# A gMLP and sliding-window decoder trunk: first loads and first products in another order, spatial gating and row sums moved

## The chip, the cores and the metric

The kernel runs on one core of a Trainium2 chip. Its engines, as the profile names them: PE (TensorE) multiplies matrices and adds into banks of PSUM, PEld is PE's load of the stationary operand, DVE (VectorE) works elementwise on two operands, ACT (ScalarE) computes functions and copies, POOL (GpSimd) does elementwise work and masks, SP (SyncE) issues most transfers between HBM and SBUF. ACT issues a few. Each engine runs its instructions strictly in the order in which they were put, and waits for the others by semaphores.

The metric is the device time of one execution in microseconds (us), smaller is better. The times of the kernel before are given as a median of three runs.

## The reference

One batch of 1024 tokens, width 1024, all in float32, passes through two layers. What matters of it:

```python
def gmlp_mixer(h, w_in, ln_g, ln_b, w_s, b_s, w_out):       # layer 1
    u, v, z = jnp.split(h @ w_in, 3, axis=-1)               # 1024 -> 3 x 2048
    u = gelu(u)
    v = layer_norm(gelu(v), ln_g, ln_b)
    v = v.reshape(bsz, 8, 128, 8, 256)                      # chunks, tokens, groups, channels
    w_causal = where(tril, w_s, 0)
    s = einsum('gts,bnsgc->bntgc', w_causal, v) + b_s       # a 128x128 matrix per group
    return (u * s * silu(z)) @ w_out

# layer 1: h = x + rms_norm(gmlp_mixer(rms_norm(x)))
# then k, v = rms_norm(h) @ w_k, rms_norm(h) @ w_v
# layer 2: windowed attention with sinks and ALiBi, a SiLU gate, w_out, rms_norm, residual
```

The change touches layer 1 alone: the product that gives v, and the part that gives u and z with the spatial product s.

## The kernel before

**Products.** Each float32 operand is split into a high part of type fp32r and the low rest, also fp32r (ACT makes the high part, DVE the low). A product is the sum of three matmuls, high by high, high by low, low by high: `mm3` (lines 226 to 229), 128 rows by 512 columns into one PSUM bank. On top of that the layer's products are cut in 2 x 2 blocks, and the four blocks are got by seven products of sums of blocks, numbered m = 1 to 7. `T[m]` is the token side's operand of product m, in a high and a low tile; the weights' side is split piece by piece as it arrives.

**Stage 1, `v_layer` (lines 343 to 573, some 0 to 155 us).** It takes 28 steps n of a product m and half u of the inner dimension, in the order m = 1, 2, 5, 6, 7, 4, 3. A step multiplies two slices k of 128 rows (kk = 0, 1) with four slices t of 128 tokens, each a call of `mm3`, so 24 matmuls. The sums of product 1 stand in four banks `vb`, those of product 2 in four banks `vc`. Two steps ahead `prep` loads and splits. The first steps are written out by hand (lines 460 to 487): the first weight piece `r0` (`raw_v`) is loaded in halves of 512 columns, the token slices `xa` 0 and 1 each on its own, then 2 and 3 together, then the second weight piece `r1_`. ACT (line 471) writes the high part of `T[1]`, POOL (line 472) that of the weights, DVE the two low parts (lines 473 and 475). Behind them come the splits of slices 2 and 3 (`split_scaled`, lines 108 to 110) and of `r1_` (`split`, lines 104 to 106), and then the next operands. Line 386 (`t_prep`, m = 5) scales `xa` in place on ACT and is held behind the split of `r1_`. The piece called `whi<-vraw` in the trace (line 105, step 4) follows on ACT, and on DVE its low part (line 106).

**Stage 2, `uz_layer` (lines 576 to 812, some 155 to 497 us).** u and z are computed for eight groups g of 256 channels, a "quad" q for u (zz = 0) and one for z (zz = 1), 16 quads. A quad is seven products into three banks, `ub` (products 1, 2 in `ua`, 6, 7, 4) and `uc` (5 and 3). Its weights (`raw_uz`, two transfers) are split in three lots, `whi_g`/`wlo_g`, and two named `uzhilo_g` (from sums `f`, which POOL makes at line 264 when they are loaded). A group's z quad also holds the spatial product: `spatial(g, i, j)` (lines 680 to 690) multiplies four slices of the normalised v, `vg`, with the masked matrix `wc`, plain float32, 128x128 (tile `sp`, four matmuls in the program, each two passes in the trace). DVE then applies gain and offset `t1` (line 687) and multiplies u by it (line 264, `uz_slots<-uz_slots,sp`). `group_consts(g)` (lines 660 to 673) loads the next group's `vg` on SP (1 MB) and computes the row sums of `wc` in a bank `rb`: DVE clears it (line 667), PE multiplies with ones (line 668), DVE makes two tiles `t` of offsets (line 672). `normalise` (line 678) then subtracts the mean from `vg` and scales, eight slices on DVE.

The banks for `sp`, `rb`, `uc` and `ua` are four, in turn. The tile `vg` exists once: its next load waits until the matmuls of `sp` have read it. At the end of a product, `scale` multiplies with the tokens' factor `bc` on DVE (line 264, `uz_slots<-uz_slots,bc`), SiLU or GELU follows on ACT (lines 694 and 778), and the result goes out in transfers `td`. Between the steps of stage 2 a generator `presum` (lines 814 to 846) prepares sums of the second layer's weights: two loads `presum_raw`, five POOL additions (line 832), ACT and DVE splits (lines 840, 841), and a store `od` of 640 KB.

**What sets the order.** The program is written as a sequence of calls; a scheduler that knows dependencies sorts the instructions of each engine by a priority that follows this sequence, and lets some go ahead. What is tied by `tc.keep_in_program_order` stays as written. So a call at another place in the code can move instructions of several engines.

## Time and profile before

| | |
|---|---|
| median of 3 runs | 1029.4 us (1029.36 to 1029.69) |
| the profiled execution: its own time | 1029.93 us |
| its span, first to last instruction | 1028.2 us |
| PE busy | 1019.6 us, 99% of the span |
| DVE busy | 767.7 us, 75% |
| ACT busy | 512.9 us, 50% |
| POOL busy | 255.3 us, 25% |
| mean granted TensorE clock | 0.998 |

Busy is the time in which an engine has an instruction in execution. A matmul's record of 0.39 us overlaps the next one's: in the steady run the starts of two matmuls of 128x512 lie 0.227 us apart (22 rows from 12.20 to 16.96 us, without a wait). In the rows of the timeline, the number in front is the start in us, the next the duration, `xN` the number of instructions put together in the row, and a bracket says how long the engine had stood idle before it and what ended that.

### The profile page before, as it was taken

How to read it: one execution, taken by the hardware profiler on the slowest of the kernel's cores; microseconds unless marked ns; L12 is line 12 of the kernel's file. 1: busy time of each engine (PE TensorE's matmuls, PEld its weight loads, DVE VectorE, ACT ScalarE, POOL GpSimd, SP SyncE). 2: the span in 40 equal slices, each digit the busy share in tenths (PEclk: the TensorE clock that was granted, in tenths of full speed). 3: DMA queues.
4: the chain of work that ended last, by engine and by line, in shares of the span. 5: the costliest groups of instructions: out<-in, count | busy, mean ns of one | idle time of the engine just before them, and what ended most of it. 6: DMA issues, size and time to landing. Idle time of an engine off the chain costs nothing.

```text
span 1028.2 us, 14492 instructions
## 1 busy us (share of the span) xinstructions
PE 1019.6 (99%) x5186; PEld 837.6 (81%) x5186; DVE 767.7 (75%) x1317; ACT 512.9 (50%) x1013; POOL 255.3 (25%) x251
## 2 busy tenths in 40 slices
PE   9999999999999999999999999999999999999997
PEld 7888888888888888888888888888997777777776
DVE  6997467888888888988787678555147557877986
ACT  6694443645445444455445455344126345544752
POOL 0010004374653746634200000000000112225421
PEclk9999999999999999999999999999999999999999
DMA  8788243545544455556998652997135444415564
GB/s 310 269 294 294 103 167 113 160 154 170 190 158 154 150 162 193 166 169 227 324 386 319 206 188 69 328 374 274 53 120 199 149 150 163 144 52 191 214 250 177
DMA packets 117416, 203.83 MB, mean 198 GB/s; under 512 B 7776, under 2 KB 59872, under 8 KB 117344
## 3 DMA queue, kind: packets, MB, share of 16 engines
q1 hardware_dynamic: 112512, 193.17, 54.6%
q10 hardware_dynamic: 4512, 8.68, 2.4%
q8 instruction: 41, 0.67, 0.3%
q0 software_dynamic: 320, 1.05, 0.3%
q14 instruction: 31, 0.25, 0.1%
HBM read 142.05 MB, written 60.82 MB: 197 GB/s over the span
## 4 chain that ended last, share of the span: by engine, by line
PE 97%; POOL 1%; DMA 1%; issue 0%; DVE 0%; ACT 0%; SPq 0%; DVEq 0%; POOLq 0%; ACTq 0%
PE qz L227 6%; PE qz L229 6%; PE qz L228 6%; PE ub L227 6%; PE ub L229 6%; PE ub L228 6%; PE oc L227 3%; PE oc L229 3%; PE oc L228 3%; PE uc L227 3%; PE ob L228 3%; PE ob L227 3%; PE uc L229 3%; PE uc L228 3%; PE ob L229 3%; PE sp L685 3%
## 5 line engine op out<-in xcount | busy, mean ns | idle before, releaser
L1208 ACT ACTIVATE pr<-pr,mx 128x129 f32<-128x129 f32 x128 | 50.2, 394 | 58.5 <-DVE mx L1202 58.3
L227 PE MATMUL qz<-n_hi,whi_w 128*128 128x512 f32 x192 | 77.1, 402 | 0.0
L229 PE MATMUL qz<-n_hi,wlo_w 128*128 128x512 f32 x192 | 74.9, 390 | 0.0
L228 PE MATMUL qz<-n_lo,whi_w 128*128 128x512 f32 x192 | 74.9, 390 | 0.0
L110 DVE SCALAR_TENSOR_TENSOR wlo_w<-raw_w,gn,whi_w 128x512 fp32r<-128x512 f32 x40 | 28.7, 748 | 51.0 <-ACT whi_w L109 43.8
L832 POOL TENSOR_TENSOR presum<-presum_raw 128x128 f32<-128x128 f32 x80 | 41.6, 553 | 92.4 <-DMA od<-presum 85.5
L109 ACT ACTIVATE whi_w<-raw_w,gn 128x512 fp32r<-128x512 f32 x40 | 27.1, 717 | 65.4 <-PE pv L229 30.4
L106 DVE TENSOR_TENSOR uzhilo_g<-f,uzhilo_g 128x1024 fp32r<-128x1024 f32 x31 | 45.7, 1473 | 12.7 <-ACT uzhilo_g L105 12.7
L841 DVE TENSOR_TENSOR presum<-presum 128x128 fp32r<-128x128 f32 x80 | 50.6, 674 | 2.7 <-ACT presum L840 2.7
L227 PE MATMUL ub<-T,whi_g 128*128 128x512 f32 x128 | 50.8, 397 | 0.0
L227 PE MATMUL ub<-T,uzhilo_g 128*128 128x512 f32 x128 | 50.5, 394 | 0.0
L1229 POOL TENSOR_SCALAR_AFFINE_SELECT pc<-pc 128x1024 f32<-128x1024 f32 x16 | 20.1, 1259 | 122.1 <-DVE wlo_w L110 109.2
L229 PE MATMUL ub<-T,wlo_g 128*128 128x512 f32 x128 | 50.0, 390 | 0.0
L264 POOL TENSOR_TENSOR f<-raw_uz 128x512 f32<-128x512 f32 x15 | 20.3, 1354 | 119.4 <-DMA raw_uz<-in_wuz_in_dram 104.2
L229 PE MATMUL ub<-T,uzhilo_g 128*128 128x512 f32 x128 | 49.9, 390 | 0.0
L228 PE MATMUL ub<-T,whi_g 128*128 128x512 f32 x128 | 49.8, 389 | 0.0
L228 PE MATMUL ub<-T,uzhilo_g 128*128 128x512 f32 x128 | 49.8, 389 | 0.0
L227 PE MATMUL uc<-T,uzhilo_g 128*128 128x512 f32 x124 | 48.8, 394 | 0.0
L228 PE MATMUL uc<-T,uzhilo_g 128*128 128x512 f32 x124 | 48.4, 390 | 0.0
L229 PE MATMUL uc<-T,uzhilo_g 128*128 128x512 f32 x124 | 48.3, 389 | 0.0
L105 ACT ACTIVATE whi_g<-raw_uz 128x1024 fp32r<-128x1024 f32 (+1 forms) x31 | 26.4, 852 | 41.7 <-PE ub L228 13.8
L105 ACT ACTIVATE uzhilo_g<-f 128x1024 fp32r<-128x1024 f32 x31 | 32.7, 1055 | 27.6 <-PE uc L229 21.7
(408 smaller groups left out, 3228.4 us busy)
## 6 DMA issues: line engine op xcount, KB each, us to landing
raw_uz<-in_wuz_in_dram SPq DMA_DIRECT2D x32, 512.0 KB, 3.6
orawP2a<-td SPq DMA_DIRECT2D x28, 512.0 KB, 4.3
td<-uz_slots SPq DMA_DIRECT2D x52, 256.0 KB, 2.2
od<-presum SPq DMA_DIRECT2D x16, 640.0 KB, 4.0
raw<-in_wv_in_dram SPq DMA_DIRECT2D x17, 512.0 KB, 5.0
vg<-vd SPq DMA_DIRECT2D x8, 1024.0 KB, 5.6
orawP2b<-in_wo_a_dram SPq DMA_DIRECT2D x16, 512.0 KB, 7.5
raw_w<-in_wqz_dram SPq DMA_DIRECT2D x16, 512.0 KB, 5.8
```

The source lines that it names most:

```text
L105: nc.scalar.activation(hi, src, AF.Copy)
L106: nc.vector.tensor_tensor(lo, src, hi.bitcast(F32), ALU.subtract)
L109: nc.scalar.activation(hi, src, AF.Copy, scale=g)
L110: nc.vector.scalar_tensor_tensor(lo, src, g, hi.bitcast(F32), ALU.mult, ALU.subtract)
L227: nc.tensor.matmul(out, lhsT=a_hi, rhs=b_hi, start=start, stop=False, skip_group_check=True)
L228: nc.tensor.matmul(out, lhsT=a_hi, rhs=b_lo, start=False, stop=False, skip_group_check=True)
L229: nc.tensor.matmul(out, lhsT=a_lo, rhs=b_hi, start=False, stop=stop, skip_group_check=True)
L264: (eng or nc.vector).tensor_tensor(out, a, b, op)
L685: nc.tensor.matmul(psv[:, n], lhsT=d["vg"][:, 4 * j + n, i * P:(i + 1) * P], rhs=d["wc"], start=n == 0, stop=n == 3, skip_group_check=True)
L832: tc.keep_in_program_order(nc.gpsimd.tensor_tensor(o, a, b, op))
L841: tc.keep_in_program_order(nc.vector.tensor_tensor(t[:, k], lo[k], hi.bitcast(F32), ALU.subtract))
L1208: nc.scalar.activation(pr[:, i], pr[:, i], AF.Exp, bias=mx[:, i:i + 1], scale=-1.0, accum_out=dn[:, i:i + 1])
```

## The change

Four edits, all in layer 1.

1. The head of stage 1 loads in the order weight half 0, slice 0, weight half 1, slice 1, then `r1_` half 0, slice 2, `r1_` half 1, slice 3: eight transfers of 256 KB, where there were four of 256 KB and two of 512 KB in another order. The high part of `T[1]` for slices 0 and 1 is written by ACT in halves of 256 columns. The splits of `r1_` and of slices 2 and 3 alternate.
2. In steps n = 0 and 1 the matmuls of one slice k run part by part: first high by high for all four t, then the second part for all four, then the third. From n = 2 on the order is that of before (the sort by t gives it).
3. The four spatial products of a group stand together, behind product 6 of the z quad. Before, two stood there and two behind product 5.
4. `group_consts` only loads `vg`. The row sums, a new function `row_sums`, are taken right behind the four spatial products for the next group (and once at the start for group 0).

```diff
--- before.py
+++ after.py
@@ -462,25 +462,27 @@
         load(r0[:, 0:512], wv_in[0, 0][:, 0:512])
         xload(xa[:, 0], 0, 0, 0, 1)
         nc.scalar.activation(small[:, 4:5], ones[:, 0:1], AF.Gelu_apprx_tanh)
+        load(r0[:, 512:1024], wv_in[0, 0][:, 512:1024])
         xload(xa[:, 0], 0, 0, 1, 1)
-        load(r0[:, 512:1024], wv_in[0, 0][:, 512:1024])
-        xload(xa[:, 0], 0, 0, 2, 2)
+        r1_ = raws.take("v1")
+        for k in range(2):
+            load(r1_[:, k * 512:(k + 1) * 512], wv_in[0, 1][:, k * 512:(k + 1) * 512])
+            xload(xa[:, 0], 0, 0, 2 + k, 1)
         p0 = pieces.take("v0")
         for k in range(2):
             cs = slice(k * 512, k * 512 + 512)
-            nc.scalar.activation(T[1][0][:, k], xa[:, 0, k], AF.Copy, scale=g(0, k))
+            for ts_ in (slice(0, 256), slice(256, 512)):
+                nc.scalar.activation(T[1][0][:, k, ts_], xa[:, 0, k, ts_], AF.Copy, scale=g(0, k))
             nc.gpsimd.tensor_copy(p0[0][:, cs], r0[:, cs])
             nc.vector.scalar_tensor_tensor(T[1][1][:, k], xa[:, 0, k], g(0, k), T[1][0][:, k].bitcast(F32),
                                            ALU.mult, ALU.subtract)
             nc.vector.tensor_tensor(p0[1][:, cs], r0[:, cs], p0[0][:, cs].bitcast(F32), ALU.subtract)
         ready[0] = p0
-        r1_ = load(raws.take("v1"), wv_in[0, 1])
-        for k in range(2, 4):
-            split_scaled(T[1][0][:, k], T[1][1][:, k], xa[:, 0, k], g(0, k))
         ready[1] = pieces.take("v1")
         for k in range(2):
             cs = slice(k * 512, k * 512 + 512)
             split(ready[1][0][:, cs], ready[1][1][:, cs], r1_[:, cs])
+            split_scaled(T[1][0][:, 2 + k], T[1][1][:, 2 + k], xa[:, 0, 2 + k], g(0, 2 + k))
         first_split.append(list(nc.cur_bb.bb.instructions)[-2])
         xload(xb, 1, 0, 0, 2)
         prep(2)
@@ -503,10 +505,11 @@
             for kk in range(2):
                 k = 2 * u + kk
                 cs = slice(kk * 512, kk * 512 + 512)
-                for t in range(4):
-                    ts_ = slice(t * P, (t + 1) * P)
-                    mm3(ps[t], T[m][0][:, k, ts_], T[m][1][:, k, ts_], hi[:, cs], lo[:, cs],
-                        first and k == 0, k == HT - 1)
+                by_part = [(i, t) for i in range(3) for t in range(4)]
+                for i, t in by_part if n < 2 else sorted(by_part, key=lambda a: a[1]):
+                    a, b = (T[m][i // 2][:, k, t * P:(t + 1) * P], (hi, lo, hi)[i][:, cs])
+                    nc.tensor.matmul(ps[t], lhsT=a, rhs=b, start=first and k == 0 and i == 0,
+                                     stop=k == HT - 1 and i == 2, skip_group_check=True)
             if n >= 2 and (Q, m, u) != (0, 2, 1):
                 prep(n + 2)
             if n >= len(steps) - 3:
@@ -662,6 +665,9 @@
             d["vg"] = vg = big.tile([P, NB, 256], F32, tag="P1_2", name=f"vg{g}")
             src = vd[g // 2][:, :, g % 2 * 256:g % 2 * 256 + 256]
             nc.sync.dma_start(out=vg, in_=src.rearrange("n p c -> p n c"))
+
+        def row_sums(g):
+            d = grp[g]
             wc, bsb = d["wc"], d["bsb"]
             ps = bank("s", f"rb{g}")[:, 0:P]
             nc.vector.memset(ps, 0.0)
@@ -726,6 +732,7 @@
         four = big.tile([P, 4, TH], F32, tag="P1_3", name="uz_slots4")
         slots += [more[:, i] for i in range(6)] + [four[:, i] for i in range(4)]
         group_consts(0)
+        row_sums(0)
         fetch(1)
         prev = None
         for q in range(len(quads) + 1):
@@ -778,8 +785,11 @@
                     tc.keep_in_program_order(nc.scalar.activation(pc[at], pc[at], AF.Gelu_apprx_tanh))
             step(sums_b)
             if zz:
-                spatial(g, 0, 0)
-                spatial(g, 0, 1)
+                for i in range(2):
+                    for j in range(2):
+                        spatial(g, i, j)
+                if g + 1 < G:
+                    row_sums(g + 1)
                 if not last:
                     finish(g, 0, 0)
             else:
@@ -791,9 +801,6 @@
             step(sums_b)
             prep2(q + 1)
             fetch(q + 2)
-            if zz:
-                spatial(g, 1, 0)
-                spatial(g, 1, 1)
             product(q, 7, b, False)
             c[1, 1] = slot()
             copy(c[1, 1], b)
```

How this moves the rows of the engines, at three places. A number behind a tile's name (`sp_2970`) tells apart the tiles of one name, and differs between the two programs.

ACT at the head, `T_133` being the high part of `T[1]`, and `T_164` or `T_168` that of `T[2]`. First before, then the change:

```order
L471 ACTIVATE T_133<-xa,gn 128x512 x2
L109 ACTIVATE T_133<-xa,gn 128x512 x2
L105 ACTIVATE whi_v_157<-raw_v_151 128x512 x2
L386 ACTIVATE xa<-xa,gn 128x512
L109 ACTIVATE T_164<-xb,gn 128x512 x2
L386 ACTIVATE xa<-xa,gn 128x512
L105 ACTIVATE vhi_171<-raw_02_169 128x1024
L386 ACTIVATE xa<-xa,gn 128x512
```

```order
L475 ACTIVATE T_133<-xa,gn 128x256 x4
L105 ACTIVATE whi_v_157<-raw_v_140 128x512
L109 ACTIVATE T_133<-xa,gn 128x512
L105 ACTIVATE whi_v_157<-raw_v_140 128x512
L109 ACTIVATE T_133<-xa,gn 128x512
L386 ACTIVATE xa<-xa,gn 128x512 x2
L109 ACTIVATE T_168<-xb,gn 128x512 x2
L386 ACTIVATE xa<-xa,gn 128x512
L105 ACTIVATE vhi_175<-raw_02_173 128x1024
L386 ACTIVATE xa<-xa,gn 128x512
```

The scaling of line 386, which stood behind the split of `r1_`, still does, and `r1_` now comes between the last slices of `xa`; ACT has four smaller pieces for the first two slices, and the last piece of `T_133` is now behind the split of `r1_`. In the rows that follow, the fourth L386 stood behind the four copies `vslot`, and now stands ahead of them.

DVE in group 4 of stage 2, from the clearing of `rb` to the multiplication with `bc` (`vg_3051` and `vg_3062` are the v of group 5, which is loaded here; `sp_3019`, `sp_3026` and `sp_2981`, `sp_2988`, `sp_2995` are spatial products of group 4). Before, then the change:

```order
L667 MEMSET rb_3053 128x128
L106 TENSOR_TENSOR uzhilo_g_10_3010<-f_3006,uzhilo_g_10_3010 128x1024
L687 SCALAR_TENSOR_TENSOR sp_3019<-sp_3019,gn,t_41_2707 128x512
L687 SCALAR_TENSOR_TENSOR sp_3026<-sp_3026,gn,t_41_2707 128x512
L264 TENSOR_TENSOR uz_slots_1333<-uz_slots_1333,sp_3019 128x512
L264 TENSOR_TENSOR uz_slots<-uz_slots,sp_3026 128x512
L672 SCALAR_TENSOR_TENSOR t_50_3056<-rb_3053,gn,bsb_2824 128x128
L264 TENSOR_TENSOR uz_slots_1333<-uz_slots_1333,uc_2987 128x512
L672 SCALAR_TENSOR_TENSOR t_51_3058<-rb_3053,gn,bsb_2824 128x128
L264 TENSOR_TENSOR uz_slots_1333<-uz_slots_1333,bc 128x512
L678 TENSOR_SCALAR vg_3051<-vg_3051,mv,ve 128x256 x7
L264 TENSOR_TENSOR uz_slots_1333<-uz_slots_1333,uz_slots 128x512
```

```order
L673 MEMSET rb_3002 128x128
L264 TENSOR_TENSOR uz_slots<-uz_slots 128x512
L678 SCALAR_TENSOR_TENSOR t_50_3005<-rb_3002,gn,bsb_2828 128x128
L678 SCALAR_TENSOR_TENSOR t_51_3007<-rb_3002,gn,bsb_2828 128x128
L848 TENSOR_TENSOR presum<-presum 128x128 x3
L106 TENSOR_TENSOR uzhilo_g_10_3035<-f_3031,uzhilo_g_10_3035 128x1024
L684 TENSOR_SCALAR vg_3062<-vg_3062,mv,ve 128x256
L264 TENSOR_TENSOR uz_slots_1337<-uz_slots_1337,uc_3012 128x512
L684 TENSOR_SCALAR vg_3062<-vg_3062,mv,ve 128x256
L264 TENSOR_TENSOR uz_slots_1337<-uz_slots_1337,bc 128x512
L684 TENSOR_SCALAR vg_3062<-vg_3062,mv,ve 128x256 x6
L264 TENSOR_TENSOR uz_slots_1337<-uz_slots_1337,uz_slots 128x512
```

Before, `rb` was cleared between the two pairs of spatial products, and all of `normalise` stood behind the multiplication with `bc`. Now all four gains of the spatial products and their four multiplications stand ahead of the clearing, and the first slice of `normalise`, which needs the load of `vg`, stands ahead of the addition of `uc` and the multiplication with `bc`.

On SP, in the same place, before and now:

```order
L101 DMA raw_uz_1_3017<-in_wuz_in_dram 128x1024
L700 DMA td_98<-uz_slots 128x512
L664 DMA vg_3051<-vd_96 128x8x256
L651 DMA wc_3173<-in_ws_t_dram 128x128
L653 DMA bsb_3175<-in_bs_dram 128x128
```

```order
L101 DMA raw_uz_1_3042<-in_wuz_in_dram 128x1024
L667 DMA vg_3062<-vd_96 128x8x256
L654 DMA wc_3177<-in_ws_t_dram 128x128
L706 DMA td_98<-uz_slots 128x512
L656 DMA bsb_3179<-in_bs_dram 128x128
```

The load of `vg` and that of the `wc` of the group after it stand ahead of a store `td1` (`td_98`), which they followed before.

PE around the row sums of group 5, again before and now (`ub_2878` and `ub_2882` are the same product 7 of group 4's z quad):

```order
L228 MATMUL ub_2878<-T_445,uzhilo_g_9_2946 128x512
L229 MATMUL ub_2878<-T_445,uzhilo_g_9_2946 128x512
L668 MATMUL rb_3053<-wc_2822,ones 128x128
L227 MATMUL ub_3065<-T_133,whi_g_10_2919 128x512
L228 MATMUL ub_3065<-T_133,whi_g_10_2919 128x512
```

```order
L229 MATMUL ub_2882<-T_449,uzhilo_g_9_2950 128x512
L227 MATMUL ub_2882<-T_449,uzhilo_g_9_2950 128x512
L674 MATMUL rb_3002<-wc_2826,ones 128x128
L228 MATMUL ub_2882<-T_449,uzhilo_g_9_2950 128x512
L229 MATMUL ub_2882<-T_449,uzhilo_g_9_2950 128x512
```

Before, `rb` followed twelve matmuls of product 7 that stood behind the second pair of spatial products. Now it stands behind the four spatial products, twelve matmuls `uc` and four of `ub`, ahead of the other eight.

## The prediction

> **What bounds the kernel now.** I read the page's busy times first, then the windows by stage, then what PE waits for.
>
> ```profile
> PE 1019.6 (99%) x5186; PEld 837.6 (81%) x5186; DVE 767.7 (75%) x1317; ACT 512.9 (50%) x1013; POOL 255.3 (25%) x251
> ...
> 0.00:45.00 45.00, 43.28 (x192) 35.69 (x193) 35.86 (x44) 26.55 (x38) 1.43 (x6) 1.00 0.85 299
> ...
> 187.00:497.00 310.00, 309.93 (x1501) 260.93 (x1500) 268.37 (x395) 152.78 (x255) 159.45 (x158) 1.00 0.55 176
> 497.00:1028.00 531.00, 524.40 (x2870) 424.07 (x2868) 362.31 (x735) 254.48 (x599) 76.64 (x66) 1.00 0.58 205
> ...
> PE vb L227 <- ACT T L471: 0.4, 1, 0.4
> ```
>
> In the windows the first pair is the stretch and its length, then the busy time of PE, PEld, DVE, ACT and POOL, the clock, the DMA share and GB/s. PE is idle 1.72 us of the first 45, 0.07 us of the 310 in which u and z are made, and 6.6 us in the second layer, which the change does not touch. So the change can win what the first products lose around their start, and next to nothing elsewhere, while any new wait in the u and z stage stands on PE's path at once. PE's clock is full. The question is which waits it makes.
>
> **The head.** The rows of PE, ACT, DVE in the first 28 us:
>
> ```profile
> 5.70 0.47 PE L227 MATMUL vb<-whi_v,T 128*128 128x512 f32 x1 [0.44 <-ACT T L471]
> 9.11 0.50 PE L228 MATMUL vb<-wlo_v,T 128*128 128x512 f32 x1 [0.15 <-DVE wlo_v L475]
> 17.19 0.39 PE L227 MATMUL vc<-vhi,T 128*128 128x512 f32 x1
> 28.18 0.47 PE L227 MATMUL vc<-whi,T 128*128 128x512 f32 x1
> ...
> 2.54 0.20 ACT L464 ACTIVATE small<-ones 128x1 f32<-128x1 f32 x1
> 4.84 0.72 ACT L471 ACTIVATE T<-xa,gn 128x512 fp32r<-128x512 f32 x1 [1.90 <-DMA xa<-in_xT_dram]
> 8.97 1.34 ACT L109 ACTIVATE T<-xa,gn 128x512 fp32r<-128x512 f32 x2 [2.21 <-DMA xa<-in_xT_dram]
> 10.28 1.15 ACT L105 ACTIVATE whi_v<-raw_v 128x512 fp32r<-128x512 f32 x2
> 19.10 1.06 ACT L105 ACTIVATE whi<-vraw 128x1024 fp32r<-128x1024 f32 x1
> ...
> 27.35 2.47 DVE L541 TENSOR_TENSOR vslot<-vslot,vc 128x512 f32<-128x512 f32 x4
> ```
>
> PE starts when the first high part is done. In halves, the first piece of 256 columns lies between the 0.20 us of one column and the 0.72 of 512; with half of the difference, 0.46. PE starts 0.26 us earlier. The 48 matmuls of the first two steps take 11.49 us (5.70 to 17.19), at 0.227 each they would take 10.90: 0.6 us are lost to the second weight half, which lands last (the wait at 9.11). In the change it lands ahead of slice 1, and part by part the low parts are wanted four matmuls later. So PE would be 0.85 us earlier at 17.19.
>
> It doesn't keep that. The matmul at 28.18 waits for DVE to free the banks (the four additions from 27.35), DVE there works through a chain that begins with `whi` at 19.10, and ACT has no gap from 8.97 to 19.10. The bytes ahead of the last first-step load are the same, so ACT starts the last piece of `T` where it now starts `whi_v`, at about 10.28. From there the work to `whi` is one `T` (0.66) where two halves of `whi_v` stood (1.06 from start to start): 0.4 us less, and nothing less if the last quarter lands 0.4 later for being alone. DVE's chain thus moves 0 to 0.4 us. I take **−0.25**; the ends are −0.85 and, if the halves land slowly (next), +1.9.
>
> A rule of the Trainium skill speaks against the halves. In this trace:
>
> ```profile
> GB/s 0 0 64 228 355 339 156 172 262 404 396 412 407 410 426 412 382 370 393 391 399 401 401 412 382 432 426 377 382 232 254 393 134 25 82 153 393 432 366 167
> ```
>
> (the first 30 us in slices of 0.75). The small first loads, around 4.5 to 6 us, moved at 156 to 172 GB/s, the large ones behind them at about 400. 256 KB more in each class cost 1.6 us against 0.65. If the four new halves moved as slowly as the first ones, two pairs in place of two whole loads, the last would land about 1.9 us later (2 x 0.95): that is a rival below. The Trainium skill, "DMA: Bandwidth & Descriptors", section "Rules for kernel authors", asks for 1 MiB or more in one transfer for full bandwidth, and its "Anatomy of one DMA" gives a cost of about 2.0 us per transfer whatever its size; an estimate by that page, two more transfers, would be 4 us if none overlapped. The 400 GB/s of queued 512 KB loads here show that most of it overlaps.
>
> **The spatial products, on PE.**
>
> ```profile
> 187.94 1.95 PE L685 MATMUL sp<-wc,vg 128*128 128x128 f32 x16
> 189.96 0.40 PE L229 MATMUL uc<-T,uzhilo_g 128*128 128x512 f32 x1
> ```
>
> Sixteen passes and one matmul take 2.02 us (187.94 to 189.96). A pass, from the block of 16 whose last record is 0.275 long, is (1.95 − 0.275)/15 = 0.112, and 16 x 0.112 + 0.227 is 2.02. Changing between the two kinds costs nothing then, and joining two blocks saves nothing: **0**.
>
> **A group in its normal course** (group 1, block of `sp` at S = 229.68):
>
> ```profile
> 229.68 1.95 PE L685 MATMUL sp<-wc,vg 128*128 128x128 f32 x16
> 230.76 1.65 DVE L687 SCALAR_TENSOR_TENSOR sp<-sp,gn,t 128x512 f32<-128x512 f32 x2 [0.37 <-PE sp L685]
> ...
> 229.22 4.14 SPq L101 DMA_DIRECT2D raw_uz<-in_wuz_in_dram  x2
> ...
> 244.43 0.39 PE L227 MATMUL ua<-T,whi_g 128*128 128x512 f32 x1
> ...
> DMA to landing us min/median/max: 5.3/5.6/7.9
> ```
>
> Two orders become new waits. First, PE's `rb` now stands at S + 3.40 (two blocks) + 0.09 + 16 x 0.227 = S + 7.12, and DVE clears its bank only behind four gains and four multiplications. Second, DVE's first `vg` slice now stands ahead of the addition of `uc` and the multiplication with `bc`; behind that, ACT's SiLU and copy of `ua` free what PE needs for `ua`. All of it hangs on the landing of `vg`, which the last row times from its issue.
>
> The durations of DVE come from group 4:
>
> ```profile
> 355.56 1.95 PE L685 MATMUL sp<-wc,vg 128*128 128x128 f32 x16
> 353.99 2.44 POOL L832 TENSOR_TENSOR presum<-presum_raw 128x128 f32<-128x128 f32 x5 [2.43 <-DMA od<-presum]
> 357.39 1.23 DVE L106 TENSOR_TENSOR uzhilo_g<-f,uzhilo_g 128x1024 fp32r<-128x1024 f32 x1 [2.94 <-ACT uzhilo_g L105]
> 358.53 1.41 DVE L687 SCALAR_TENSOR_TENSOR sp<-sp,gn,t 128x512 f32<-128x512 f32 x2
> 359.85 0.68 DVE L264 TENSOR_TENSOR uz_slots<-uz_slots,sp 128x512 f32<-128x512 f32 x1
> 364.20 1.40 DVE L687 SCALAR_TENSOR_TENSOR sp<-sp,gn,t 128x512 f32<-128x512 f32 x2
> 365.52 1.27 DVE L264 TENSOR_TENSOR uz_slots<-uz_slots,sp 128x512 f32<-128x512 f32 x2
> 366.97 0.68 DVE L264 TENSOR_TENSOR uz_slots<-uz_slots,uc 128x512 f32<-128x512 f32 x1
> 367.83 0.81 DVE L264 TENSOR_TENSOR uz_slots<-uz_slots,bc 128x512 f32<-128x512 f32 x1
> 370.19 2.03 DVE L678 TENSOR_SCALAR vg<-vg,mv,ve 128x256 f32<-128x256 f32 x6 [1.55 <-DMA vg<-vd]
> 357.44 4.14 SPq L101 DMA_DIRECT2D raw_uz<-in_wuz_in_dram  x2
> 362.22 0.38 SPq L664 DMA_DIRECT2D vg<-vd  x1
> 369.61 0.58 ACT L267 ACTIVATE ua<-ub 128x512 f32<-128x512 f32 x1
> 370.31 0.43 PE L227 MATMUL ua<-T,whi_g 128*128 128x512 f32 x1
> ```
>
> From the first gain to the end of the clearing: two gains 1.32 (358.53 to 359.85), a multiplication 0.7, two gains 1.32, three multiplications 1.9, clearing 0.17: 5.4 us. In group 1 the gains start at S + 1.08, the clearing ends at S + 6.5, 0.6 us ahead of `rb`. `vg` is issued behind the second `raw_uz`, at S + 3.7 (229.22 + 4.14 = 233.36). With 5.6 us it lands at 239.0. From its landing to the end of the copy of `ua`: a slice, the addition, a slice (0.3 + 0.6 + 0.3), and from the start of the multiplication with `bc` to the end of the copy 2.36 (367.83 to 369.61 + 0.58): 3.6 us, so 242.6, where PE wants `ua` at 244.43. A normal group costs **0**. At 7.9 us it would be 244.9, 0.45 late: the upper end.
>
> **Group 4** is late: POOL waited for the store `od`, ACT and DVE followed, and the gains start at S + 2.97 (358.53). Before, nothing came of it, since the copy of `ua` still ended 0.1 us ahead of PE (370.19 against 370.31). Now the clearing ends at 358.53 + 5.4 = 363.95 and `rb` stands at 355.56 + 7.12 = 362.68: PE waits 1.3 us. `vg` is issued at 357.44 + 4.14 = 361.6, since `raw_uz` waits for POOL, 0.6 earlier than before. Before it took at most 7.97 us (362.22 to 370.19, where DVE's wait ended); now the store `td1` of 256 KB is no longer ahead, 0.65 us at 400 GB/s. It lands at 361.6 + 7.3 = 368.9, the copy of `ua` ends at 372.5, and PE, which stood at 370.31, starts at 372.55: **+2.25**, the 1.3 of `rb` contained. With 5.3 us only `rb` counts, +1.3, with 7.9 it is +2.85.
>
> **Group 5**, gains too at S + 3.22:
>
> ```profile
> 397.56 0.83 PE L685 MATMUL sp<-wc,vg 128*128 128x128 f32 x6
> 400.78 1.41 DVE L687 SCALAR_TENSOR_TENSOR sp<-sp,gn,t 128x512 f32<-128x512 f32 x2
> ```
>
> If all of it moves with PE, `rb` waits 400.78 + 5.4 − (397.56 + 7.12) = 1.5 us; if DVE keeps its time while PE comes 2.25 later, 0. I take **+0.4**, nearer to nothing, because what was late was a transfer and not PE.
>
> **The sum:** −0.25 + 0 + 2.25 + 0.4 = +2.4. The profiled execution took 1029.93, so 1032.33; it stands 0.53 above the median, which gives **1031.8 us**.
>
> **The rivals.** About 0.2%, 2.06 us, is what a measurement of this kernel tells from no change: faster is below 1027.3, slower above 1031.46.
>
> *The forecast*, late `vg` and `rb` in group 4: own range 1030.7 to 1033.3, chance 0.42.
>
> *Not slower:* the store `od` ahead of group 4, for which POOL stood idle 2.43 us, lands in the usual time,
>
> ```profile
> od<-presum SPq DMA_DIRECT2D x16, 640.0 KB, 4.0
> ```
>
> (4.0 us, the page's median): the gains of group 4 start near S + 1.1, all loads of `vg` land in time, and only the head remains: 1029.4 − 0.25, up to −0.85: 1028.5 to 1029.2. For it: before, the lateness of groups 4 and 5 cost PE nothing, so the agreement of three runs doesn't tell whether it recurs. Against: two of eight groups show it. Decides: whether DVE's gains start before S + 1.7. Chance 0.25.
>
> *Only `rb`:* `vg` hides, `rb` waits in group 4: −0.25 + 1.3 to 1.7, 1030.5 to 1030.9. For it, the median of 5.6 us; against, 7.97 in this very group. Chance 0.13.
>
> *`vg` late everywhere:* each of the six other groups pays up to 0.45: 2.4 + 2.7, 1034.5. Against it, only one load of eight took 7.9 us. Chance 0.12.
>
> *Slow halves at the head* (the rule above): the last load 1.9 us later, ACT's chain with it: 2.4 + 0.25 + 1.9, 1033.9. Chance 0.05.
>
> The remaining 0.03 is for a gain that no row shows. Two thirds of the forecast's chance lie above 1031.46, with the last two rivals this gives 0.47 for slower, 0.50 within, 0.03 faster. The range, 1028.7 to 1034.4, leaves out the ends of the first and fourth rival.
>
> **What would show it.** Right: the first matmul near 5.45, no wait near 9, `whi` of step 4 at 18.7 to 19.1; a wait of `rb` on DVE's clearing of 1 us or more in group 4 and none in groups 1 and 2; a wait of PE's `ua` on ACT's copy in group 4, with DVE idle ahead of its first `vg` slice until the DMA. Wrong: gains of group 4 near S + 1.1 (then the second rival), DVE idle on `vg` in every group (the fourth), PE idle at 10 to 17 us (the fifth), or PE's blocks of 32 passes not 3.5 us long.

## The result, and the profile after

The change makes the kernel slower. The median of six runs of the changed kernel is 1035.09 us (1034.67 to 1037.59), that of six runs of the one before 1029.63; the ratio is 1.0057, with a 95% interval of 1.0045 to 1.0070. Forecast were 1031.8 us, 2.4 more than before, and a range of 1028.7 to 1034.4: the loss is 5.5 us, and the time lies 0.7 us beyond the range. The profiled execution of the changed kernel took 1036.39 us, 6.46 more than that of before. One execution of e2 below took 1273.95 us at a granted clock of 0.752 and is left out of the medians and ratios.

The page of the changed kernel, and its view of what PE waits for (in us: total, number of times, longest):

```profile
PE 1022.3 (99%) x5186; PEld 837.6 (81%) x5186; DVE 772.8 (75%) x1317; ACT 513.3 (50%) x1015; POOL 260.4 (25%) x251
```

```profile
PE ua L227 <- ACT ua L267: 2.1, 3, 0.9
PE warm L1056 <- DVE small L93: 1.1, 1, 1.1
PE rb L674 <- DVE rb L673: 0.8, 1, 0.8
PE vb L511 <- ACT T L475: 0.7, 1, 0.7
PE vb L511 <- ACT ve L267: 0.6, 1, 0.6
```

The matmuls `warm` stand at the very start, at 1.12 us, and wait in the same way in the kernel before. Of the others, the waits of `ua` and `rb` are new and stand in the u and z stage, the waits of `vb` in stage 1. The window of the u and z stage (the first pair is the stretch and its length, then busy PE, PEld, DVE, ACT, POOL, the clock, DMA share and GB/s):

```profile
187.00:497.00 310.00, 307.01 (x1479) 256.22 (x1478) 269.73 (x388) 149.05 (x251) 165.04 (x161) 1.00 0.53 169
```

PE idles 3.0 us of these 310, where it idled 0.07. The clock is full in both.

Where the time goes is best seen from PE's own place. The table gives the start of the first matmul of `ua` behind the spatial products of each group, as the timeline of PE has it. The last three columns belong to experiments below.

| group | before | changed | difference | e10 | e3 | e11 |
|---|---|---|---|---|---|---|
| 0 | 202.47 | 204.66 | 2.19 | 202.45 | 201.93 | 202.58 |
| 1 | 244.43 | 246.91 | 2.48 | 244.56 | 244.31 | 244.53 |
| 2 | 286.39 | 289.20 | 2.81 | 286.83 | 286.26 | 286.47 |
| 3 | 328.35 | 331.49 | 3.14 | 329.10 | 328.20 | 328.42 |
| 4 | 370.31 | 375.76 | 5.45 | 373.56 | 371.00 | 370.37 |
| 5 | 412.55 | 418.05 | 5.50 | 417.19 | 412.94 | 412.31 |
| 6 | 454.66 | 461.21 | 6.55 | 459.51 | 454.89 | 454.26 |

Without a wait a group takes 41.96 us (244.43 − 202.47). Against the kernel before, the changed kernel loses about 0.3 us in groups 1, 2 and 3, 2.3 in group 4 and 1.05 in group 6. Of the 2.19 at group 0, 0.6 are its own, and some 1.6 us lie ahead of it, in stage 1 (its block of `sp` starts at 189.52, before at 187.94); the experiment e1, with the same first loads, doesn't show them.

**A normal group.** Group 1 in the timeline of the changed kernel. Its block of `sp` starts at S = 231.78. The columns are start, duration, engine and line; a bracket says how long the engine stood idle before and on what.

```profile
231.78 3.73 PE L691 MATMUL sp<-wc,vg 128*128 128x128 f32 x32
235.98 0.39 SPq L667 DMA_DIRECT2D vg<-vd  x1
240.54 1.22 DVE L106 TENSOR_TENSOR uzhilo_g<-f,uzhilo_g 128x1024 fp32r<-128x1024 f32 x1
241.90 1.29 POOL L264 TENSOR_TENSOR f<-raw_uz 128x512 f32<-128x512 f32 x1 [6.38 <-DVE uzhilo_g L106]
243.26 1.30 POOL L264 TENSOR_TENSOR f<-f,raw_uz 128x512 f32<-128x512 f32 x1
242.56 0.77 DVE L684 TENSOR_SCALAR vg<-vg,mv,ve 128x256 f32<-128x256 f32 x1 [0.80 <-DMA vg<-vd]
243.25 0.68 DVE L264 TENSOR_TENSOR uz_slots<-uz_slots,uc 128x512 f32<-128x512 f32 x1
243.85 0.86 DVE L684 TENSOR_SCALAR vg<-vg,mv,ve 128x256 f32<-128x256 f32 x1
244.63 0.68 DVE L264 TENSOR_TENSOR uz_slots<-uz_slots,bc 128x512 f32<-128x512 f32 x1
246.28 0.58 ACT L267 ACTIVATE ua<-ub 128x512 f32<-128x512 f32 x1
246.91 0.50 PE L227 MATMUL ua<-T,whi_g 128*128 128x512 f32 x1
```

Three things differ from the forecast for this group. SP issues `vg` at S + 4.20, not S + 3.7. The load lands at 242.56, 6.58 us later, not 5.6. And the two slices of `normalise` take 0.69 and 0.78 us from start to start (242.56 to 243.25, 243.85 to 244.63) where 0.3 each were taken, because each ends just behind one of POOL's two additions: POOL's end at 241.90 + 1.29 = 243.19, the slice at 243.33; POOL at 244.56, the slice at 244.71. From landing to the end of ACT's copy of `ua` it is 4.30 us (242.56 to 246.86), not 3.6. The landing is late by 1.46 against S (S + 10.78, forecast 239.0 − 229.68 = S + 9.32), the rest by 0.7, and the spare time was 1.83 (242.6 to 244.43): 0.3 us of wait, as the table shows.

POOL's additions did not lie beside the slices before. They now wait for DVE's split of line 106 (241.76), which has moved on DVE from S + 5.9 to S + 8.8. In the kernel before (S = 229.68) the same rows were

```profile
235.54 1.23 DVE L106 TENSOR_TENSOR uzhilo_g<-f,uzhilo_g 128x1024 fp32r<-128x1024 f32 x1 [0.25 <-ACT uzhilo_g L105]
237.10 1.29 POOL L264 TENSOR_TENSOR f<-raw_uz 128x512 f32<-128x512 f32 x1 [4.10 <-DMA raw_uz<-in_wuz_in_dram]
238.47 1.29 POOL L264 TENSOR_TENSOR f<-f,raw_uz 128x512 f32<-128x512 f32 x1
241.64 1.71 DVE L678 TENSOR_SCALAR vg<-vg,mv,ve 128x256 f32<-128x256 f32 x5 [0.54 <-DMA vg<-vd]
```

so POOL was done before the first slice began. The tile `vg` over the whole execution, in the changed kernel:

```profile
L684 DVE TENSOR_SCALAR vg<-vg,mv,ve x64: 396/404/1386, 168.7 to 461.2; 128x256 f32<-128x256 f32 x64
  DMA vg<-vd: 8.4, 7
DMA to landing us min/median/max: 5.5/6.7/8.0
```

A slice now takes up to 1386 ns, where the median is 404; the median load takes 6.7 us from issue to landing, where it was 5.6.

The landing and the slices don't simply add up. In groups 1, 2 and 3 the first slice starts at S + 10.79, S + 11.15 and S + 10.57, and the copy of `ua` ends at S + 15.08 in all three. POOL's additions, from S + 10.12 to S + 12.78 in each, set that time, and the landing counts only by falling among them. In group 6 it falls to the start of the second addition, so the first slice ends behind that one (456.70 + 1.39 = 458.09, POOL at 457.94), and the copy of `ua` ends at S + 15.99:

```profile
456.65 1.29 POOL L264 TENSOR_TENSOR f<-f,raw_uz 128x512 f32<-128x512 f32 x1
456.70 1.39 DVE L684 TENSOR_SCALAR vg<-vg,mv,ve 128x256 f32<-128x256 f32 x1 [1.55 <-DMA vg<-vd]
```

**Group 4.**

```profile
358.63 3.73 PE L691 MATMUL sp<-wc,vg 128*128 128x128 f32 x32
361.40 1.41 DVE L693 SCALAR_TENSOR_TENSOR sp<-sp,gn,t 128x512 f32<-128x512 f32 x2
366.85 0.46 PE L674 MATMUL rb<-wc,ones 128*128 128x128 f32 x2 [0.84 <-DVE rb L673]
371.50 1.13 DVE L684 TENSOR_SCALAR vg<-vg,mv,ve 128x256 f32<-128x256 f32 x1 [1.81 <-DMA vg<-vd]
375.76 0.50 PE L227 MATMUL ua<-T,whi_g 128*128 128x512 f32 x1 [0.94 <-ACT ua L267]
```

The gains are late (S + 2.77), `rb` waits, `vg` comes last and PE waits for `ua`: forecast and found. (The slice of 1.13 us, too, has an addition of POOL beside it.)

### The profile page after: what moved, and what is told of

Same layout as the page of the kernel before. It is cut to its first block, busy times and chain, and to the rows that moved or that the text cites. A ratio compares the mean times of both kernels' runs of the same rounds, so it can differ in the third digit from the quotient of the medians.

```text
span 1034.7 us, 14496 instructions
## 1 busy us (share of the span) xinstructions
PE 1022.3 (99%) x5186; PEld 837.6 (81%) x5186; DVE 772.8 (75%) x1317; ACT 513.3 (50%) x1015; POOL 260.4 (25%) x251
## 3 DMA queue, kind: packets, MB, share of 16 engines
q0 software_dynamic: 320, 1.05, 0.3%
## 4 chain that ended last, share of the span: by engine, by line
PE 89%; DVE 4%; ACT 2%; DMA 2%; issue 1%; POOL 1%; DVEq 0%; POOLq 0%; ACTq 0%
PE qz L227 6%; PE qz L229 6%; PE qz L228 6%; PE vb L511 5%; PE ub L227 5%; PE ub L228 5%; PE ub L229 5%; PE vc L511 4%; PE oc L227 3%; PE oc L229 3%; PE oc L228 3%; PE ob L229 3%; PE ob L228 3%; PE ob L227 3%; PE uc L228 3%; PE uc L229 3%
## 5 line engine op out<-in xcount | busy, mean ns | idle before, releaser
L839 POOL TENSOR_TENSOR presum<-presum_raw 128x128 f32<-128x128 f32 x80 | 47.6, 627 | 84.3 <-DMA od<-presum 77.5
L848 DVE TENSOR_TENSOR presum<-presum 128x128 fp32r<-128x128 f32 x80 | 52.7, 707 | 1.6 <-ACT presum L847 1.6
L511 PE MATMUL vb<-whi,T 128*128 128x512 f32 x144 | 45.4, 390 | 0.1
```

The lines of the kernel that those rows point to most:

```text
L511: nc.tensor.matmul(ps[t], lhsT=a, rhs=b, start=first and k == 0 and i == 0, stop=k == HT - 1 and i == 2, skip_group_check=True)
L839: tc.keep_in_program_order(nc.gpsimd.tensor_tensor(o, a, b, op))
L848: tc.keep_in_program_order(nc.vector.tensor_tensor(t[:, k], lo[k], hi.bitcast(F32), ALU.subtract))
```

## The experiments

Each diff is against the kernel that is named with it. Ratios are to the kernel before, run beside it on the same chip. None of the kernels leaves out any of the computation.

**e1: edits 1 and 2 alone; e2: edits 3 and 4 alone.**

> The first two edits alone (load order, halves, part by part), groups as before. PE in the changed kernel was 0.57 us late by 39 us and 1.6 us late from 51 us on, where it waited for ACT's copies behind a late load of x. If the head is a loss of its own, this kernel takes 1.6 us more than before (1.2 to 2.0) and PE waits near 9 and near 51 us. Rival: the late load near 43 us was a chance of that execution; then it takes 0.6 us more, or nothing. The forecast's own value was 0.25 us less than before.

> The spatial products together and the row sums moved, the head as before. If head and groups add up, this kernel takes 3.9 us more than before (5.5 less 1.6), from waits of PE for the copy of ua in groups 0 to 6 and for the clearing of rb in group 4. Rival: without the later head the groups' transfers fall otherwise and only group 4 waits, about 2.3 us more.

Measured: e1 1029.30 us against 1029.47, ratio 0.9997 (0.9988 to 1.0005); e2 1034.66, ratio 1.0052 (1.0038 to 1.0066). No loss of the head can be seen (−1.2 to +0.5 us by its interval), and e2's loss of 5.2 us is, within the intervals, that of the full change. The head's rows in e1:

```profile
7.21 0.91 ACT L475 ACTIVATE T<-xa,gn 128x256 fp32r<-128x256 f32 x2 [1.49 <-DMA xa<-in_xT_dram]
16.46 0.39 PE L511 MATMUL vc<-vhi,T 128*128 128x512 f32 x1
28.19 0.47 PE L511 MATMUL vc<-whi,T 128*128 128x512 f32 x1 [0.41 <-DVE vslot L544]
```

PE stands 0.73 us earlier at the first `vc` (17.19 before) and at the same place at 28.19: what the head wins is lost at the chain through `whi`, as forecast. In the profiled execution of the full change, with the same loads, slice 1 came 1.5 us later:

```profile
8.69 0.91 ACT L475 ACTIVATE T<-xa,gn 128x256 fp32r<-128x256 f32 x2 [2.96 <-DMA xa<-in_xT_dram]
```

I had expected e1 to show that loss, and it doesn't. Nor do the medians: e1's −0.2 and e2's +5.2 make 5.0, and the full change measured 5.5 (4.6 to 7.2 by its interval), with its profiled execution 1.3 us above its own median. So the 1.6 us of stage 1 belong to that execution, as far as these runs tell.

**e3: the first slices of `normalise` held behind the multiplication with `bc`.** As e2, and on DVE, by order alone:

```diff
                 nc.vector.tensor_scalar(vg[:, n], ...)
+                if scaled:
+                    tc.add_manual_dep(<this>, scaled[-1], NoSync)
...
             scale(c[1, 1], 1)
+            scaled.append(<this>)
```

> As e2_groups, with the first slices of normalise held behind the multiplication with bc on DVE, as before. If the wait for the load of vg ahead of that multiplication is the cause of PE's waits for ua, these go in every group and only the wait of rb in group 4 is left: 1.0 to 1.3 us more than before. Rival: the copy of ua is late because the split of uzhilo_g now stands ahead of the addition of uc; then PE's waits of about 0.3 us in groups 1 to 3 stay.

Measured: 1030.86, ratio 1.0015 (1.0006 to 1.0024), 3.8 us less than e2. PE has no wait for `ua` left. What remains is

```profile
PE rb L671 <- DVE rb L670: 0.9, 2, 0.6
```

So 3.8 of the 5.2 us hang on two DVE rows that stand ahead of the addition of `uc` and the multiplication with `bc`, and the rest on `rb`. In the table, e3 loses 0.4 us in group 1 and 0.8 in group 4, and nothing elsewhere.

**e4: POOL's additions held back.** As e2, and the addition `s1` of the quad after next waits for the multiplication with `bc`, so that POOL is away while the slices run:

```diff
             add(s1, a21, a22, ALU.add, eng)
+            if q - 2 in scaled:
+                tc.add_manual_dep(<this>, scaled[q - 2], Sync)
```

> As e2_groups, with POOL's two additions f that run beside the vg slices held back until the multiplication with bc of the same group is done. In the changed kernel the first two vg slices ended within 0.1 us of the end of each of these additions and took 0.4 to 1.4 us where they take 0.34 alone. If DVE waits there for POOL, both slices take 0.34 us, the copy of ua ends about 0.9 us earlier, the waits for ua of groups 1 to 3 go (0.3 us each) and those of groups 0, 4 and 6 shrink by about 0.6 each: 2.0 to 2.8 us less than e2_groups. Rival: the landing of vg alone sets it; then no difference to e2_groups beyond 0.3 us.

Measured: 1038.84, ratio 1.0092 (1.0078 to 1.0106), slower than e2 by 4 us. The rows in question, however, became short:

```profile
241.92 0.41 DVE L684 TENSOR_SCALAR vg<-vg,mv,ve 128x256 f32<-128x256 f32 x1 [1.26 <-DMA vg<-vd]
242.25 0.68 DVE L264 TENSOR_TENSOR uz_slots<-uz_slots,uc 128x512 f32<-128x512 f32 x1
242.85 0.41 DVE L684 TENSOR_SCALAR vg<-vg,mv,ve 128x256 f32<-128x256 f32 x1
243.17 0.68 DVE L264 TENSOR_TENSOR uz_slots<-uz_slots,bc 128x512 f32<-128x512 f32 x1
244.09 1.30 POOL L264 TENSOR_TENSOR f<-raw_uz 128x512 f32<-128x512 f32 x1 [8.99 <-DVE uz_slots L264]
244.83 0.58 ACT L267 ACTIVATE ua<-ub 128x512 f32<-128x512 f32 x1
```

With POOL away a slice takes 0.33 us from start to start, and from landing to the copy's end it is 3.49 us (241.92 to 245.41): the 3.6 of the prediction. The total went the other way because the held additions made the split behind them late, and with it the gains of the next groups:

```profile
PE rb L674 <- DVE rb L673: 6.3, 6, 1.3
```

Six groups now pay at `rb` what one paid. The run confirms what POOL does to the slices; its total was forecast at 2.0 to 2.8 us less than e2, so that forecast failed, and it says nothing on what the slices cost.

**e5: the four spatial products together, row sums where they were; e6: row sums moved, spatial products in two pairs as before.**

Against e2, which has the head of before:

```diff
@@ e5
         def group_consts(g):      # loads vg and takes the row sums, as before
             if zz:
                 for i in range(2):
                     for j in range(2):
                         spatial(g, i, j)
-                if g + 1 < G:
-                    row_sums(g + 1)
@@ e6
+                spatial(g, 0, 0); spatial(g, 0, 1)      # behind product 6
...
+                spatial(g, 1, 0); spatial(g, 1, 1)      # behind product 5
+                if g + 1 < G:
+                    row_sums(g + 1)
```

> The third edit alone: the four spatial products together, the row sums called where they were (with the load of the next vg), head as before. In its order vg's first two slices again stand ahead of the addition of uc, and rb behind all of the two products. If joining the products is what put the wait for vg ahead, it costs what the waits for ua cost in e2_groups, 3.5 to 4.5 us more than before, with no wait of rb. Rival: the row sums' move makes the order, then it is within 0.5 us of before.

> The fourth edit alone: the row sums right behind the spatial products, which stay in two pairs, head as before. DVE keeps the order of before but for the second offset tile t, which goes ahead of the addition of uc. By the theory that the joined products carry the loss it is within 0.5 us of before; by the rival, that the row sums do, 1 to 4 us more.

Measured: e5 1038.30 against 1029.43, ratio 1.0088 (1.0074 to 1.0102); e6 1030.79, ratio 1.0008 (0.9997 to 1.0019). PE's waits in e5:

```profile
PE ua L227 <- ACT ua L267: 3.9, 7, 1.5
PE rb L668 <- DVE rb L667: 1.1, 1, 1.1
```

All seven groups wait for `ua` in e5, none in e6, where DVE keeps the order of before around `normalise`. So it is the joining of the spatial products that brings the slices forward. (Likely since `vg` is read out earlier and its next load goes earlier, so that the scheduler takes the slices for due; that is argued, not shown.) With the row sums left behind them, two slices and one offset tile `t` stand ahead of `bc`, and the loss of 8.9 us is larger than in e2, and twice what I had expected. Moving the row sums alone costs one wait of `rb` in group 4 in the trace (1.29 us); the single times run from 1029.0 to 1032.12, and the interval (−0.3 to +2.0 us) does not tell this from nothing.

**e7: the slices in another form.** As e2, with `normalise` written as an operation on two tensors (`scalar_tensor_tensor` with `ve` broadcast):

```diff
-                nc.vector.tensor_scalar(vg[:, n], vg[:, n], mv[:, n, 0:1], ve[:, n:n + 1], ALU.subtract, ALU.mult)
+                nc.vector.scalar_tensor_tensor(vg[:, n], vg[:, n], mv[:, n, 0:1],
+                                               ve[:, n:n + 1].broadcast_to([P, 256]), ALU.subtract, ALU.mult)
```

> As e2_groups, with normalise written as an operation of two tensors (the factor of the token broadcast along the row) and not of one tensor with two scalars; same order on every engine. In the changed kernel the first two slices ended with POOL's additions f. If a one-tensor operation of DVE waits while POOL works and one of two tensors does not, as line 264's multiplications beside POOL suggest, the slices take 0.4 us each, the copy of ua ends 0.3 to 0.9 us earlier, the waits for ua of the groups that have 0.16 to 0.25 go, and it takes 1.5 to 2.5 us less than e2_groups (1032.4 to 1033.4). Rival: the landing of vg alone sets it, then it is within 0.5 us of e2_groups.

Measured: 1033.03, ratio 1.0039 (1.0026 to 1.0052), single times from 1032.33 to 1035.19. The slice still ends with POOL's addition (240.31 + 1.29 = 241.60, the slice at 241.88):

```profile
240.31 1.29 POOL L264 TENSOR_TENSOR f<-raw_uz 128x512 f32<-128x512 f32 x1 [6.32 <-DVE uzhilo_g L106]
240.69 1.19 DVE L681 SCALAR_TENSOR_TENSOR vg<-vg,mv,ve 128x256 f32<-128x256 f32 x1 [0.51 <-DMA vg<-vd]
```

So both forms wait, and the form is not the cause. The median lies where it was expected if the form were the cause (1032.4 to 1033.4); that is luck, as the trace shows. Why it is 1.6 us below that of e2 I can't say: the profiled execution, 1035.19, lost as much as e2.

**e8: the split `whi` of step 4 ahead.** As e1, with that split put ahead of the four copies `vslot` on ACT, to see whether the head's gain can be kept:

```diff
                 prep(3)
+                first_split.append(<the ACT half of that split>)
...
                         copy(a1[t], ps[t])
+                        tc.add_manual_dep(<this>, first_split[1], NoSync)
```

(and the split of `T` from `tch`, and the last two scalings of line 386, held in the same way).

> As e1_head, with ACT's split of the fourth step's weights (whi from vraw) ahead of the copies vslot, of the split of T from tch and of the last two scalings of line 386. In e1_head PE came 0.73 us earlier out of the first two steps and lost it again at 28.19 to DVE's additions, whose chain begins with that split at 19.18. If that chain is what takes the head's gain, the wait at 28 goes, PE is 0.5 us earlier there, and it takes 0.5 us less than e1_head (1028.8). Rival: the transfers of stage 1 set the pace behind it, and the 0.5 us are lost again before 95 us.

Measured: 1030.98, ratio 1.0015 (1.0006 to 1.0024). The wait at 28 us is gone, and the loss is 1.5 us where a gain was expected. A new wait stands behind it, which is part of that:

```profile
61.49 0.50 PE L513 MATMUL vb<-whi,T 128*128 128x512 f32 x1 [0.58 <-ACT vslot L267]
```

The head's 0.7 us can't be had by this order of ACT.

**e9: POOL's additions in halves; e10: e2 once more beside it; e11: e5 with `normalise` held as in e3.**

```diff
@@ e9 = e2 and
-            add(s1, a21, a22, ALU.add, eng)
-            add(s2, s1, a11, ALU.subtract, eng)
+            for o, x, y, op in ((s1, a21, a22, ALU.add), (s2, s1, a11, ALU.subtract)):
+                for h in (slice(0, 256), slice(256, 512)):
+                    add(o[:, h], x[:, h], y[:, h], op, eng)
```

> As e2_groups, with POOL's first two additions f of a quad written as four of 256 columns, so that none lasts longer than 0.7 us; DVE's order in the groups unchanged. In e2_groups the first vg slice ended 0.1 us behind the first of these additions and the second behind the second, and the copy of ua 4.2 to 4.6 us behind the landing of vg, where it was 3.5 when POOL was kept away. If a vg slice waits for the addition that POOL has begun, a slice waits at most 0.7 us now, the copy of ua ends 0.6 to 0.7 us earlier in each group, the waits for ua of 0.16 to 0.25 go and those of about 1.1 us halve: 1.5 to 2.5 us less than e10_groups_again. Rival, vg's landing alone: no difference.

> The same kernel as e2_groups, for comparison on the same chip: 1034.9, within 0.7 us.

> As e5_merge (the spatial products together, row sums called where they were), with normalise held behind the multiplication with bc. If the two waits found (for vg ahead of that multiplication, for the clearing of rb behind the products) are all that the joining costs, the waits for ua go; rb stands 2.3 us later on PE than in e3_vg_behind, but its clearing stands 2.5 us later on DVE, so that it waits when the gains start later than S + 1.7, as before: 1.3 us in group 4 and little else. 0.8 to 1.8 us more than before, 7 us less than e5_merge. Rival: the joined products cost on their own; then more than 3 us stay.

Measured, against 1029.51: e10 1034.78, ratio 1.0051 (1.0039 to 1.0064), so e2's loss repeats; e9 1032.62, ratio 1.0030 (1.0020 to 1.0040); e11 1029.62, ratio 0.9997 (0.9988 to 1.0006).

e11 is the clearest of all. It keeps the joined spatial products and holds only the slices back. The 8.9 us of e5 vanish and every group takes 41.94 to 41.95 us (table). In e5's trace groups 1, 2, 3 and 6 take 0.6 us more than 41.96 each, and groups 4 and 5, where POOL and a load were late, 2.5 and 1.8; in e11 group 4 was on time, so that part of the gain may not be due to the slices. POOL's additions still meet a DVE row, now the multiplication with `bc`, which takes 1.53 us instead of 0.68:

```profile
240.50 1.53 DVE L264 TENSOR_TENSOR uz_slots<-uz_slots,bc 128x512 f32<-128x512 f32 x1
```

That costs nothing here, since no row on the way to `ua` waits for the landing of `vg` any more: the copy of `ua` ends at 243.58, and PE wants it at 244.53.

e9 saved about as much as I had expected (2.2 us against e10), but not where. In groups 1, 2 and 6 the copy of `ua` ended no earlier against S than in e10 (S + 15.14 to S + 15.29, e10 S + 15.08 to S + 15.16). What it saved is group 4 (2.1 us), whose gains were on time in it, and group 5 behind it (1.3). Group 3 of e9 shows something else: there the first slice stood at S + 9.90, ahead of POOL's additions, and the copy ended at S + 13.38, with POOL at work behind it. So an early landing takes the wait away as well as POOL's absence does. Ahead of group 4, SP issues the store `od` and POOL waits for it; e10, then e9:

```profile
349.40 0.37 SPq L848 DMA_DIRECT2D od<-presum  x1
354.48 2.62 POOL L836 TENSOR_TENSOR presum<-presum_raw 128x128 f32<-128x128 f32 x5 [3.88 <-DMA od<-presum]
```

```profile
349.97 0.37 SPq L849 DMA_DIRECT2D od<-presum  x1
354.16 2.59 POOL L837 TENSOR_TENSOR presum<-presum_raw 128x128 f32<-128x128 f32 x5 [1.20 <-DMA od<-presum]
```

5.1 us from issue to POOL's start against 4.2. In e11 and e12 group 4 was on time as well; in ten of the other traces, that of before included, its gains start at S + 2.5 or later. So the second rival of the prediction, the store in its usual time, does occur, in other kernels than the change itself. What sets the store's time wasn't tried and stays open, and e9 can't be read as a test of the slices.

**e12: edits 1 and 2 with e11.**

> The first three edits, with normalise held behind the multiplication with bc, and the row sums called where they were. e1_head measured 0.2 us less than before, e11_merge_held 0.1 us more. If the two add up and no other cost is in the change, it is within 0.5 us of before (1029.0 to 1030.0): the loss of the changed kernel is then in the order of DVE and in the early row sums. Rival: head and joined products spoil each other's transfers; more than 1 us above before.

Measured: 1029.38 against 1029.34, ratio 1.0002 (0.9993 to 1.0011). PE's only waits of 0.2 us or more are those of `warm` at the start and of `o` in the second layer. With the slices held, edits 1 to 3 together cost nothing and bring nothing; no kernel here beats the one before.

## Why the prediction was wrong

**The step that failed is "A normal group costs 0".** The prediction saw the chain (landing of `vg`, slice, addition of `uc`, slice, `bc`, copy, `ua`) and gave it 1.8 us of spare time. Both terms in it were undersized:

- *The landing.* 5.6 us was the median of loads that SP issued, most of them, some 3 us behind the 512 KB of `raw_uz` (in group 1 before at S + 6.5). In the change `vg` is issued right behind them, and loads take 6.7 us in the median (5.5 to 8.0). The issue itself was at S + 4.2 where S + 3.7 was taken. That the closeness to `raw_uz` makes a load slow is argued and not shown: in e8, where `vg` is issued as before, the median is 7.0.
- *The 3.6 us behind it.* They were summed from rows in which POOL did nothing beside the slices. With POOL's two additions there it was 4.3 us in group 1; with POOL away 3.49 (e4). The prediction never asked which POOL rows move when DVE's do: the additions wait for DVE's split of line 106, and this split was moved with the rest.

Each is smaller than the spare time; only the two together pass it. With the landing at S + 10.79 and POOL away the copy would end at S + 14.3, in time for PE at S + 14.75 (244.43 − 229.68), and with an early landing and POOL there it ended at S + 13.38 (group 3 of e9). Where the landing falls among POOL's additions the wait is 0.3 us, whatever the exact time, and 0.9 to 1.4 us more where a load that is issued later lands at the second addition (group 6 in the profile of the change, issued at S + 4.7; group 5 in e10, at S + 5.3). Holding the slices alone took 3.8 us off (e3), and all of e5's loss (e11, with group 4 on time). In the profile of the change the step is 2.6 of the 5.0 us that are lost from group 0 on: 0.6 in group 0, 0.3 each in groups 1 to 3, 1.05 in group 6. In e10, against the kernel before, it is 1.2 of 5.1 us, with 2.5 in group 4, of the kind that was forecast, and 1.4 in group 5, where 0.4 was. The rival that `vg` is late everywhere, with 1034.5 us, came nearest in the number and was given 0.12; its sign, DVE idle on `vg` in every group, is there (8.4 us, 7 times), but it had the landing and not the slices.

The Trainium skill, "SBUF — State Buffer", section "SBUF: two separate sides", says that DVE (in some modes, or with two operands in SBUF) and GpSimd share a pair of ports that one of them holds for a whole instruction while the other stands still. The traces agree: a slice that takes 0.41 us alone ends 0.14 and 0.15 us behind POOL's 1.3 us additions in group 1, and the addition of `uc`, whose second operand comes from PSUM, keeps its 0.68 us beside the second of them. That the ports are the cause is the Trainium skill's reading, and whether the slice runs in one of those modes no run here shows; the runs show that POOL's presence is the cause (e4 against e2).

**Head, −0.25:** in keeping with e1, but not shown by it. e1 took 0.2 us less, which its interval does not tell from nothing, with PE 0.73 us earlier at the first `vc` and level at 28.2, so that the trace shows 0 rather than −0.25. The rival of slow halves, +1.9 us, is refuted by e1 (0.9997, at most +0.5 us). The 4 us estimated for two more transfers from the Trainium skill, "DMA: Bandwidth & Descriptors", section "Anatomy of one DMA", don't appear; the page gives its fixed cost for transfers that GpSimd issues, and these are issued by SP.

**Spatial products, 0 on PE:** right. The 32 passes start at 231.78 and take 3.73 us to the end of the last record, which agrees with 31 x 0.112 + 0.275 = 3.75. e12 shows that they cost nothing if `normalise` stays put.

**Group 4, +2.25:** right in form, and in size (2.3 by the table) partly by luck. The gains started at S + 2.77, `rb` waited 0.84 us and started 5.45 us behind the first gain (361.40 to 366.85), for which 5.4 was forecast, and `ua` followed. The landing came 0.5 us earlier than forecast (S + 12.87, where 368.9 − 355.56 = S + 13.3 was taken), and the rows behind it took 4.2 us and not 3.6, again with POOL beside the first slice: two errors that cancel. That group 4 is late in every kernel isn't so: e9, e11 and e12 had the gains on time.

**Group 5, +0.4:** 0.05 in the profile of the change, 1.4 in e10. Group 6 lost 1.05 in the change, which was not foreseen. Late `vg` moves between these groups from one program to another.

Two small sums are off and change nothing: `rb` stands at S + 7.21 on PE (238.99 − 231.78), not at S + 7.12, and the terms of the chance for slower add up to 0.45, not 0.47.

## What to carry to other kernels

When a call moves in the program, look not only at what the moved instruction waits for but at what now stands behind it in its engine's queue: two short operations on a late load, ahead of two that were ready, cost 3.8 of 5.2 us here, and holding them back by order alone removed it. Take a load's time with its whole spread, and from loads issued in the same company, not from the median over all. And when DVE's order moves, follow POOL's rows that wait for DVE, since an operation timed alone may run beside them afterwards, at two to three and a half times its length.

## What the hardware showed that I had not expected

- DVE and POOL: a slice of 128x256 takes 0.41 us alone (0.33 from start to start) and up to 1.39 us beside POOL's additions, and is held in the other form too (e7, 1.19); the multiplication with `bc` 0.68 alone, 1.53 beside them (e11).
- A load of 1 MB issued right behind 512 KB landed 6.7 us after its issue in the median (the change), one issued mostly some 3 us behind 5.6 (before), but 7.0 in e8 with the same order of issue as before.
- The same store of 640 KB let POOL go 4.2 us after its issue in one program (e9) and 5.1 in another (e10), and with it a whole group was on time or late. What it depends on is open.
